# A hybrid retention, latent-attention and expert layer: the order of steps, heads, router, branch and last pair is changed, and the last norm is shared out differently

## The chip, the core and the metric

The kernel runs on one core of a Trainium2 chip. Its engines are TensorE (PE in the profile; its weight loads are PEld), VectorE (DVE), ScalarE (ACT), GpSimd (POOL) and SyncE (SP, which issues nearly all loads). The metric is the device time of one execution in microseconds; lower is better.

## The reference

One layer for 256 latent tokens of width 2048 and 256 context tokens, in fp32. Cut to what matters here:

```python
mod_x = split(silu(c) @ w_ada + b_ada, 6)          # modulations 0 to 5; mod_c for the context
proj = modulate(x, mod_x[0], mod_x[1]) @ w_in      # q, k, v, g, latents; for the context too
ret = retention_output(bidirectional_retention(rope(q), rope(k), v), g)   # 8 heads
att = block_attention(latent queries, latent keys and values)              # 8 heads
mix = concat([ret, att]) @ w_o
h = layer_norm(ALPHA * x + mod_x[2] * mix)
y = hier_moe(modulate(h, mod_x[3], mod_x[4]))      # 4 groups x 8 experts, each token in 2
out = layer_norm(ALPHA * h + mod_x[5] * y)
```

`hier_moe` picks one group and two experts of it for each token. The 32 experts' weights are 403 MB of fp32.

## The kernel before

The program is written as one stream of operations; a planner (priority by place in the program, with modelled durations) sets the order in which each engine issues them, except where an order is pinned. No order is pinned in the kernel before.

**Input projection (L567 to L636).** The rows of the weight are taken in six stages of 1, 1, 2, 4, 4 and 4 blocks of 128 (`STAGES`). Within a stage the ten column blocks of 512 (`NB_TO`) come as chunks of about 1 MB, in the order that `win_chunks` gives (L47); blocks 2, 3, 4, 5 and 9 are computed for latent and context tokens (four row tiles), the others for the latent ones (two). A chunk is split into a rounded high and a low part (`split_w`: ScalarE copies, VectorE subtracts, L273 and L274, two buffers), and each product is three TensorE products (L594 to L596). Chunks stream through four buffers (`st`). Between chunks run *pieces* of the product that gives modulations 0 and 1 for the next stage (`gemv_plan`, L510 to L543): one piece is one modulation's share of a chunk of rows, with its own load in `st`; the even and odd rows of modulation m go to column groups 2m and 2m+1 of one bank. They are spread over the chunks by L604.

**Modulation steps (`ada_step`, L243).** Modulations 2 to 5 are summed by VectorE: 64 steps, each a 1 MB load (`sa`, two buffers) and two operations on 128x1024 (L250). `ada_v` holds 48 of them (modulations 3, 4, 2) and `ada_g` 16 (modulation 5). `ADA_V` places them behind chunks, `ADA_V_MLA` in the attention, `ADA_G_WO` in the output projection. `ada_finish` (L210) sums modulations 3 and 4 over partitions with 16 one-column products each.

**Retention.** In the last stage k is rotated on GpSimd behind chunk 3, q on VectorE behind chunk 5, and there also all eight heads are written (`ret_tables`, `ret_head`, L347 to L408). `mla_latents` follows at chunk 8, then the norm and output of retention, then the attention.

**Output projection and router (L842 to L912).** Four blocks of 512 columns, 16 chunks. The products of the router with the not yet normalised rows are accumulated on the way (`router_part`); `router_consts` makes on GpSimd four weighted copies of the router's weights and sums them on VectorE (L810). After the last block come mean and variance, the router's logits, the choice of group and experts (L942 to L954), the places of tokens (L956 to L970), and `norms` (L925), which makes the normalised rows in high and low parts for the gather.

**Experts (L1190 to L1241).** 16 pairs. Expert weights are loaded 2 MB at a time into six buffers, five ahead (`expert_chunk`). For each expert the tokens' rows are gathered by products with 0/1 matrices (`gather_two`, L1049), multiplied by gate and up (L1071) and down (L1116), scaled by their gates in a high and a low part (`down`, L1122 and L1123), and scattered back by two products (`scatter`, L1130), multiplied by modulation 5 (L1131) and added to h (L1132). Behind the sixth pair (`pr == 5`) a branch handles experts that got more tokens than their 64 places (`overflow`, L1134); it is not taken in the profiled execution.

**Last norm (L1243 to L1254).** Statistics, then eight pieces: VectorE takes six of them in two operations each (L181, L182), ScalarE and GpSimd the two others (L184 to L186); each piece is stored when ready.

## Time and profile before

| | |
|---|---|
| time, median of 3 runs | 1685.78 us (1684.48 to 1687.98) |
| profiled execution, time | 1686.18 us |
| profiled execution, span | 1684.4 us |
| mean granted TensorE clock | 0.972 of full |
| TensorE busy (with pipelined ends) | 1521.6 us, 90% |
| VectorE busy | 919.9 us, 55% |
| ScalarE busy | 484.2 us, 29% |
| GpSimd busy | 105.9 us, 6% |
| HBM read and written | 575.8 and 2.1 MB, 343 GB/s over the span |

The span runs from the first to the last instruction of one execution. Engine shares over the whole span mix stages with different limits, so they are read by stage. A matmul's recorded duration contains its pipeline's end; the step from one start to the next is its price in a row of them.

### The profile page before, as it was taken

Reading aid. Unit: us, or ns where it says so; the run is one execution under the profiler, and the core shown is the slowest. Engines: PE = TensorE matmul, PEld = TensorE weight load, DVE = VectorE, ACT = ScalarE, POOL = GpSimd, SP = SyncE. Lnnn points to the kernel's source line nnn. Section 1 sums busy time; section 2 is a strip of 40 time slices with the busy share of each in tenths; the row PEclk is TensorE's granted clock in tenths of the full one; section 3 lists DMA queues with packets and bytes.
Section 4 is the critical chain, followed back from the end, with each engine's and each line's share of the span. In section 5 each row is a group of like instructions: output and inputs, shape, how many; then the busy total and the mean of one; then the engine's idle time right before and its main releaser. Section 6 shows DMA issues by size and latency. Waiting matters only on the chain. (4 is left out here: it accounts for less than half of the span.)

```text
span 1684.4 us, 20454 instructions
## 1 busy us (share of the span) xinstructions
PE 1521.6 (90%) x8316; PEld 919.2 (55%) x8316; DVE 919.9 (55%) x1553; ACT 484.2 (29%) x913; POOL 105.9 (6%) x91
## 2 busy tenths in 40 slices
PE   5999999988889999699999988799989989899994
PEld 4667686877768767444543543444445345336432
DVE  6877584899698768824423532432342343234238
ACT  3323232324675534431320211121122013103112
POOL 1000000053513010000000000000000000000001
PEclk8999999998999999899999999999999999999997
DMA  8787777766554579579999999999999999999993
GB/s 326 272 326 283 294 309 286 276 245 225 184 192 153 199 270 360 225 301 426 426 427 427 426 427 425 370 428 427 427 427 427 427 426 427 426 426 427 421 425 136
DMA packets 54226, 579.28 MB, mean 344 GB/s; under 512 B 6320, under 2 KB 6768, under 8 KB 8816
## 3 DMA queue, kind: packets, MB, share of 16 engines
q1 hardware_dynamic: 54000, 577.90, 84.2%
q8 instruction: 67, 1.10, 0.3%
q14 instruction: 31, 0.25, 0.0%
q0 software_dynamic: 128, 0.03, 0.0%
HBM read 575.81 MB, written 2.10 MB: 343 GB/s over the span
## 5 line engine op out<-in xcount | busy, mean ns | idle before, releaser
L1071 PE MATMUL pA<-we,xg 128*64 128x512 f32 x2048 | 468.0, 602 | 12.8 <-DMA we<-in_wexp_dram 12.8
L1071 PEld LDWEIGHTS pA<-we,xg 128*64 128x64 f32 x2048 | 140.8, 138 | 281.2 <-issue 247.6
L1116 PE MATMUL pA<-we,hT 128*64 128x256 f32 x2048 | 232.7, 382 | 17.4 <-DMA we<-in_wexp_dram 16.1
L1123 DVE SCALAR_TENSOR_TENSOR D<-pA,gcol,D 64x256 fp32r<-64x256 f32 x256 | 123.5, 482 | 176.0 <-ACT D L1122 175.3
L273 ACT CAST whi<-st 128x1024 fp32r<-128x1024 f32 (+3 forms) x130 | 125.1, 965 | 282.5 <-PE pA L596 172.5
L1116 PEld LDWEIGHTS pA<-we,hT 128*64 128x64 f32 x2048 | 147.4, 137 | 92.2 <-ACT D L1122 8.7
L595 PE MATMUL pA<-wlo,xhi 128*128 128x512 f32 (+1 forms) x480 | 188.2, 392 | 10.5 <-DVE wlo L274 10.5
L594 PE MATMUL pA<-whi,xhi 128*128 128x512 f32 (+1 forms) x480 | 185.5, 394 | 3.3 <-ACT whi L273 3.1
L596 PE MATMUL pA<-whi,xlo 128*128 128x512 f32 (+1 forms) x480 | 185.8, 387 | 0.0
L250 DVE SCALAR_TENSOR_TENSOR ada_acc<-st,c,ada_acc 128x1024 f32<-128x1024 f32 x128 | 177.5, 1406 | 8.3 <-DMA st<-in_ada_dram 8.2
L274 DVE TENSOR_TENSOR wlo<-st,whi 128x1024 fp32r<-128x1024 f32 (+2 forms) x122 | 134.6, 1112 | 57.6 <-ACT whi L273 57.1
L1122 ACT ACTIVATE D<-pA,gcol 64x256 fp32r<-64x256 f32 x256 | 120.0, 469 | 156.7 <-PE pA L1116 87.5
L1074 ACT ACTIVATE hid<-pA 128x256 f32<-128x256 f32 x32 | 12.3, 383 | 493.5 <-PE pA L1071 493.5
L1075 DVE TENSOR_TENSOR hid<-pA,hid 128x256 f32<-128x256 f32 x32 | 13.5, 423 | 219.7 <-ACT hid L1074 219.7
L594 PEld LDWEIGHTS pA<-whi,xhi 128*128 128x128 f32 x480 | 90.5, 191 | 37.5 <-ACT whi L273 17.7
L595 PEld LDWEIGHTS pA<-wlo,xhi 128*128 128x128 f32 x480 | 91.9, 191 | 31.9 <-DVE wlo L274 14.5
L1058 DVE TENSOR_SCALAR xg<-pT,modt 128x256 f32<-128x256 f32 x64 | 34.8, 544 | 131.2 <-PE pA L1071 93.7
L1131 DVE TENSOR_TENSOR pA<-pA,ada_acc 128x512 f32<-128x512 f32 x128 | 83.5, 693 | 36.8 <-PE pA L1130 36.6
L596 PEld LDWEIGHTS pA<-whi,xlo 128*128 128x128 f32 x480 | 92.0, 192 | 16.3
L1049 PE MATMUL pT<-oh,nn 128*128 128x256 f32 x512 | 80.5, 303 | 9.1 <-DVEq L1136 5.8
L1049 PEld LDWEIGHTS pT<-oh,nn 128*128 128x128 f32 x512 | 68.3, 199 | 31.7 <-issue 20.5
L1132 DVE TENSOR_TENSOR h<-pA,h 128x512 f32<-128x512 f32 x128 | 82.6, 683 | 0.8
(353 smaller groups left out, 1578.6 us busy)
## 6 DMA issues: line engine op xcount, KB each, us to landing
we<-in_wexp_dram SPq DMA_DIRECT2D x190, 2048.0 KB, 21.8
st<-in_ada_dram SPq DMA_DIRECT2D x96, 1024.0 KB, 6.7
st<-in_win_dram SPq DMA_DIRECT2D x35, 1024.0 KB, 6.7
st<-in_wo_dram SPq DMA_DIRECT2D x16, 1024.0 KB, 4.9
we<-in_wexp_dram SPq DMA_DIRECT2D x4, 1024.0 KB, 17.4
st<-in_wuq_dram SPq DMA_DIRECT2D x3, 1024.0 KB, 4.8
xn<-in_x_dram SPq DMA_DIRECT2D x2, 1024.0 KB, 6.4
xn<-in_ctx_dram SPq DMA_DIRECT2D x2, 1024.0 KB, 17.0
```

The costliest lines, as they stand in the source:

```text
L250: V.scalar_tensor_tensor(accs[m][:, sl], w[:, sl], c2[:, k, 0:1], accs[m][:, sl], op0=OP.mult, op1=OP.add)
L273: A.copy(hi, src)
L274: (eng or V).tensor_tensor(lo, src, hi, op=OP.subtract)
L594: T.matmul(banks[t][:, :wd], xh[:, sl], hi[:, kk, :wd], start=fst, stop=False)
L595: T.matmul(banks[t][:, :wd], xh[:, sl], lo[:, kk, :wd], start=False, stop=False)
L596: T.matmul(banks[t][:, :wd], xl[:, sl], hi[:, kk, :wd], start=False, stop=lst)
L1049: T.matmul(p[:, 256 * j:256 * j + width], nnh[i % 2][:, i // 2, ks], oh[:, i // 2, :width], start=(i == 0), stop=(i == 3))
L1071: T.matmul(pg[64 * cg:64 * cg + 64], xg[:, k, c0:c0 + 64], c[:, kk, 512 * cg:512 * cg + 512], start=(k == 0), stop=(k == KB - 1))
L1116: T.matmul(pd[64 * cg:64 * cg + 64, :256], hT[:, f % 2, 64 * (f // 2):64 * (f // 2) + 64], c[:, f, 256 * cg:256 * cg + 256], start=(f == 0 ...
L1122: A.activation(hl[0][rows, sl], p, AF.Copy, scale=g)
L1123: V.scalar_tensor_tensor(hl[1][rows, sl], p, g, hl[0][rows, sl], op0=OP.mult, op1=OP.subtract)
L1131: V.tensor_tensor(p, p, mod5[:, sl], op=OP.mult)
```

## The change

- Pieces of modulations 0 and 1 come as pairs: one piece loads both modulations' chunks and alternates their products. In the long stages the pieces stand behind chunks 1, 3, 4, 5 and 6. The first stage's pieces keep their written order on TensorE.
- Between the first and last stage the column blocks alternate between those without and with context.
- `ada_finish` for modulations 3 and 4 uses four 512-wide products and transposes.
- The step lists are 50 and 14 long; `ADA_V` places 23 before the last stage and 10 in it.
- k is rotated on VectorE. Tables for two heads come behind chunk 5; behind chunks 6 to 9 come two heads each, with the tables for the next two.
- The router's four sums stand behind four different chunks. From the last projection block to the last normalised part VectorE, ScalarE and TensorE issue in written order; the transposes come first, the two square roots are split from their reciprocals, the two halves of the tokens alternate in the choice, and the norm of the last three quarters comes behind the places.
- The router's weights are queued behind the last normalised part on ScalarE.
- The branch stands ahead of the sixth pair's down products; that pair's scatter and next gather follow as in every other pair.
- In the last pair `down` multiplies by gate and modulation 5 in one operation into one fp32 tile, and `scatter` is one fp32 product.
- The last norm: for columns 0 to 1023 VectorE does the first operation, TensorE multiplies by the inverse deviation (a diagonal) and adds the shift, ScalarE copies out; for the others VectorE does both. GpSimd has no part.

```diff
-ADA_V = [[0] * 10, [0] * 10, [0] * 5, [1] * 10, [1] * 10, [2] * 4 + [1] * 6]
+ADA_V = [[0] * 3, [1, 0, 0], [1, 1, 1, 0, 1], [1] * 7 + [0, 1, 1], [1] * 7 + [0, 1, 1], [1] * 10]
+GEMV_AT = (1, 3, 4, 5, 6)
...
+    elif si:
+        order = [0, 2, 1, 3, 6, 4, 7, 8, 5, 9]
...
-    ada_v = [(m, k) for m in (3, 4, 2) for k in range(KB)]
-    ada_g = [(5, k) for k in range(KB)]
+    ada_g = [(m, k) for m in (3, 4, 2, 5) for k in range(KB)]
+    ada_v = [ada_g.pop(0) for _ in range(50)]
...
-            for k in range(KB):
-                T.matmul(p[:, k:k + 1], acc[:, 128 * k:128 * k + 128], ones[:, 0:1], start=True, stop=True)
...
+            for g in range(4):
+                T.matmul(p[32 * g:32 * g + 32], ones[:, 0:32], acc[:, 512 * g:512 * g + 512], start=True, stop=True)
+            row = sa.tile([128, 2048], F32, name="st", tag="st")[:, :512]
+            A.copy(row, p)
+            p = bankT()
+            for j in range(4):
+                transpose(p[:, 128 * j:128 * j + 128], row[:, 128 * j:128 * j + 128])
...
-                c = stream(dram2(a["ada01"], base + (m * nch + j) * 128 * per * w, 128, per * w), per * w)
+                c = [stream(dram2(a["ada01"], base + (m * nch + j) * 128 * per * w, 128, per * w), per * w)
+                     for m in range(2)]
                 for kk in range(per):
                     k = j * per + kk
-                    g = 2 * m + (k % 2)
-                    T.matmul(p[32 * g:32 * g + 32, :w], csil[:, k], c[:, kk * w:kk * w + w],
-                             start=(k < 2), stop=(k >= KB - 2))
+                    for m in range(2):
+                        g = 2 * m + (k % 2)
+                        T.matmul(p[32 * g:32 * g + 32, :w], csil[:, k], c[m][:, kk * w:kk * w + w],
+                                 start=(k < 2), stop=(k >= KB - 2))
...
+            if nchunk == 10:
+                n = GEMV_AT.count(ci)
...
-                            rope(pl["k"][:, t, 512 * j:512 * j + 512], t, "ck", "sk", 4, 64, R["rt"], G)
+                            rope(pl["k"][:, t, 512 * j:512 * j + 512], t, "ck", "sk", 4, 64, R["rt"])
...
-                    for h in range(H):
+                    for h in range(2):
                         ret_tables(h)
+                if ci > 5:
+                    for h in range(2 * ci - 12, 2 * ci - 10):
                         ret_head(h)
+                        if h < H - 2:
+                            ret_tables(h + 2)
...
+                if 1 <= 4 * n + k4 <= 4:
+                    router_const(4 * n + k4 - 1, rparts[4 * n + k4 - 1])
...
+        pinned = tc.manual_schedule(engines={V.engine, A.engine, T.engine})
+        pinned.__enter__()
+        flipped = [router_flip(3, half) for half in range(2)]
         for half in range(2):
-            router_part(3, half)
+            router_rest(3, half, flipped[half])
...
+        norm_a(0, 0)
+        norm_a(1, 0)
+        V.reciprocal(hs[:, :, 1:2], hs[:, :, 1:2])
+        norm_b(0, 0)
+        norm_b(1, 0)
...
+    norm_a(1, 1)
     for t in range(2):
+        V.scalar_tensor_tensor(rk[:, t], p[:, 32 * t:32 * t + 32], 1.0, sel[:, t], op0=OP.add, op1=OP.mult)
+        normed_lo(t, 0, fs[t])
...
     oh = new_places(0)
-    norms()
+    for c in range(1, 4):
+        for t in range(2):
+            if c > 1:
+                norm_a(t, c)
+            norm_b(t, c)
+            done, f = normed(t, c)
+            normed_lo(t, c, f)
...
+            if len(hl) == 1:
+                V.scalar_tensor_tensor(hl[0][rows, sl], p, g, mod5[rows, 512 * n + 256 * cg:512 * n + 256 * cg + 256],
+                                       op0=OP.mult, op1=OP.mult)
...
+            if len(hl) == 1:
+                T.matmul(p, sT[:K, t, :].bitcast(F32), hl[0][:K], start=True, stop=True)
...
         if pr == 0:
-            router_weights()
+            with tc.issue_after(done.ins):
+                router_weights()
...
-        hl = new_D()
-        gather = pq and not final and pr != 5
+        if pr == 5:
+            overflow()
+        hl = new_D_whole() if final else new_D()
+        gather = pq and not final
...
-        if pr == 5:
-            for n in range(4):
-                scatter(hl[n], sT, 128, n)
-            hl = None
-            overflow()
...
+    for t in range(2):
+        for n in range(2):
+            p = shifted[t, n] = bankA()
+            T.matmul(p, ones[0:1], lnb[0:1, 512 * n:512 * n + 512], start=True, stop=False)
...
+    for n in range(4):
+        sl = slice(512 * n, 512 * n + 512)
+        for t in range(2):
+            hp = h[:, t, sl]
+            if n < 2:
+                T.matmul(shifted[t, n], diag[:, t], hp, start=False, stop=True)
+                A.copy(hp, shifted[t, n])
+            else:
+                affine(V, hp, mv2[:, t, 0:1], mv2[:, t, 2:3], lnw[:, sl], lnb[:, sl], None)
+            SP.dma_start(out[128 * t:128 * t + 128, sl], hp)
```

## Rows read from the trace of the kernel before

**Rows 1.** Windows: us; PE, PEld, DVE, ACT, POOL busy; clock, DMA share, GB/s.

```profile
126.00:337.00 211.00, 211.00 (x1009) 156.82 (x1008) 148.56 (x179) 61.27 (x87) 2.30 (x2) 1.00 0.75 290
337.00:404.00 67.00, 61.17 (x256) 49.12 (x255) 63.24 (x91) 20.78 (x33) 30.34 (x28) 0.95 0.68 246
404.00:490.00 86.00, 71.93 (x406) 61.45 (x405) 71.10 (x150) 59.01 (x142) 38.06 (x32) 0.92 0.55 197
490.00:600.00 110.00, 100.28 (x542) 81.76 (x540) 89.48 (x147) 58.82 (x112) 23.71 (x15) 0.98 0.49 185
...
741.00:1653.00 912.00, 838.22 (x4913) 407.40 (x4910) 329.28 (x626) 177.35 (x379) 0.00 (x0) 0.99 1.00 422
1653.00:1684.40 31.40, 7.12 (x44) 3.85 (x42) 27.45 (x44) 6.39 (x12) 5.95 (x4) 0.66 0.19 67
```

**Rows 2.** Waits of the load queue (SP): total us, times, longest.

```profile
SPq L1030 <- PE pA L1071: 554.1, 124, 31.9
...
SPq L142 <- PE pG L526: 150.6, 26, 10.9
...
SPq L1136 <- SPq L1136: 24.4, 6, 4.9
```

**Rows 3.** Timeline of TensorE, one piece and two together: start, us.

```profile
192.89 0.39 PE L595 MATMUL pA<-wlo,xhi 128*128 128x512 f32 x1
193.12 0.39 PE L596 MATMUL pA<-whi,xlo 128*128 128x512 f32 x1
193.44 1.91 PE L526 MATMUL pG<-st,csil 128*32 128x512 f32 x8
...
245.15 1.94 PE L526 MATMUL pG<-st,csil 128*32 128x512 f32 x16
```

**Rows 4.** Windows of line 526 alone, pieces of three stages, summed.

```profile
sum 159.00, PE 38.85 PEld 8.01; mean PE 12.95 PEld 2.67
```

**Rows 5.** Groups by line and shape, 0 to 600 us: busy us, mean ns.

```profile
L215 PE MATMUL pT<-ones,ada_acc 128*128 128x1 f32 x64 | 8.0, 258 | 1.0 <-ACT qk L388 1.0
...
L661 PE MATMUL pA<-st,cqall 128*128 128x512 f32 x16 | 7.2, 593 | 0.0
```

**Rows 6.** Instructions of two tiles (k, then q): ns min/median/max.

```profile
L317 POOL TENSOR_TENSOR lk<-lk,rp1p x4: 726/1222/1717, 352.2 to 377.1; 128x256 f32<-128x256 f32 x4
...
L317 DVE TENSOR_TENSOR lq<-lq,rp x4: 417/418/419, 401.4 to 409.3; 128x256 f32<-128x256 f32 x4
```

**Rows 7.** Timeline of TensorE: the heads' first wait, their last product.

```profile
408.13 0.47 PE L169 MATMUL pT<-ct,lq 128*128 128x128 f32 x1 [3.79 <-DVE lq L317]
...
458.06 0.61 PE L404 MATMUL pA<-Ssb,xq 128*128 128x128 f32 x4
```

**Rows 8.** Windows of line 250 (modulation steps) alone.

```profile
400.00:490.00 90.00, 36.52 (x25) 0.92 0.56 199
```

**Rows 9.** Timeline of TensorE, start of the output projection.

```profile
601.66 0.80 PE L853 MATMUL pA<-wlo,mix 128*128 128x512 f32 x1 [4.13 <-DVE wlo L274]
```

**Rows 10.** Timeline of VectorE, then TensorE, from projection to gather.

```profile
689.74 0.70 DVE L871 TENSOR_TENSOR pA<-pA,ada_acc 128x512 f32<-128x512 f32 x1 [1.77 <-PE pA L854]
...
700.07 0.75 DVE L182 SCALAR_TENSOR_TENSOR h<-h,hs,D 128x512 f32<-128x512 f32 x1
...
712.78 0.24 DVE L954 SCALAR_TENSOR_TENSOR sel<-ct,ef,o 128x32 f32<-128x32 f32 x1
...
713.53 4.09 PE L1049 MATMUL pT<-oh,nn 128*128 128x256 f32 x16
```

**Rows 11.** Windows: the worst 5 us of the stream, at the branch.

```profile
1070.00:1075.00 5.00, 2.98 (x14) 3.01 (x15) 2.09 (x4) 0.26 (x1) 0.00 (x0) 0.50 0.69 213
```

**Rows 12.** Groups by line on VectorE from 1640 us on.

```profile
L182 DVE SCALAR_TENSOR_TENSOR h<-h,mv,lnwb 128x512 f32<-128x512 f32 (+1 forms) x6 | 6.1, 1058 | 0.0
L1131 DVE TENSOR_TENSOR pA<-pA,ada_acc 128x512 f32<-128x512 f32 x8 | 5.6, 694 | 0.1
```

**Rows 13.** Page, load issues: KB each, median us to landing.

```profile
st<-in_wuq_dram SPq DMA_DIRECT2D x3, 1024.0 KB, 4.8
```

More of the change, by code (lines that the diff above doesn't have):

```diff
@@ L515, in gemv_plan, with piece @@
         base = sum(2 * D * n * 128 for _, n in STAGES[:si])
-        def piece(j, m):
+        def piece(j):
             def go():
@@ L540, in gemv_plan @@
         for j in range(nch):
-            pieces.append(piece(j, 0))
-            pieces.append(piece(j, 1))
+            pieces.append(piece(j))
         return pieces + [last]
@@ L558, in xhat @@
         V.tensor_tensor(lo[:, sl], full, hi[:, sl], op=OP.subtract)
-    for f in gemv_plan(0):
-        f()
-    for k in range(STAGES[0][1]):
-        xhat(k, 0)
+    with tc.manual_schedule(engines={T.engine}):
+        for f in gemv_plan(0):
+            f()
+        for k in range(STAGES[0][1]):
+            xhat(k, 0)
     SP.dma_start(rot["t"], a["consts"][:, CW:CR])
@@ L956, in tile_kernel @@
-    p = bankA()
-    T.matmul(p[:, 0:32], C("ut"), sel[:, 0], start=True, stop=True)
-    V.scalar_tensor_tensor(rk[:, 0], p[:, 0:32], 1.0, sel[:, 0], op0=OP.add, op1=OP.mult)
-    p = bankA()
-    T.matmul(p[:, 0:32], ones, sel[:, 0], start=True, stop=False)
-    T.matmul(p[:, 0:32], C("ut"), sel[:, 1], start=False, stop=True)
-    V.scalar_tensor_tensor(rk[:, 1], p[:, 0:32], 1.0, sel[:, 1], op0=OP.add, op1=OP.mult)
+    Le = [L[:, t, 8:40] for t in range(2)]
+    fs = [normed(t, 0)[1] for t in range(2)]
@@ L979, in tile_kernel @@
     oh = new_places(0)
-    norms()
+    for c in range(1, 4):
+        for t in range(2):
+            if c > 1:
[3 more added lines that the diff above has]
+            normed_lo(t, c, f)
     nnfs.close()
@@ L983, in tile_kernel @@
         f()
+    pinned.__exit__(None, None, None)
     def router_weights():
@@ L1108, in new_D, with new_D_whole @@
         return [[D2[j][:, n] for j in range(2)] for n in range(4)]
+    def new_D_whole():
+        D1 = dp.tile([128, 4, 512], F32, name="D0")
+        return [[D1[:, n]] for n in range(4)]
     def down(hT, src, hl, gcol, half, n):
```

127 lines of the change are left out of this document (73 added, 54 removed).

## The prediction

> **What bounds the kernel now.** I read the busy times by stage first [rows 1], then for each stage what the engine with the least slack waits for. From 741 to 1653 us the kernel streams expert weights: the DMA share is 1.00 at 422 GB/s, while TensorE is 838 of 912 us busy [rows 1]. Nothing in the change lessens those bytes. So this stage can only start earlier; and it starts when TensorE has worked through the first expert's gate and up product, because its reads free the ring buffers: the load queue waits longest for them [rows 2]. What is saved before 741 moves the whole stream, one for one, and so does what is saved after 1653.
>
> From 126 to 337 us TensorE is busy all 211 us at full clock while VectorE has 30% to spare and the DMA 25% [rows 1]: TensorE sets that stretch. From 337 to 600 no engine is full: TensorE 233 of 263 us, VectorE 224. There chains between engines decide, and the granted clock falls to 0.92 in the heads (404 to 490). From 600 to 691 the output projection runs, on TensorE again; from 691 to 741 first a chain of small VectorE work, then TensorE. After 1653 VectorE works 27.5 of 31.4 us.
>
> The sum is made against the profiled execution: span 1684.4 us, time 1686.2 us, which is 0.4 us above the median of the runs. It carries over as it is.
>
> **The modulation pieces.** A piece today is one modulation's share: in the last stages 8 recorded products, 1.91 us. Where the planner happened to set two pieces side by side, 16 products took 1.94 us [rows 3], since the two modulations write different column groups of one bank. The change makes every piece such a pair. The three stages with 512-wide pieces spend 38.85 us on 192 products [rows 4]; 12 pairs of 1.94 us are 23.3 us, which saves 15.6 us of TensorE. Two of the three windows lie where TensorE has no other slack; I take **-12**, bounds -16 and 0. What hides it if wrong: nothing, it is on the path; what can eat it is loading (rival 2), as a pair holds two of the four stream buffers and the queue already waits 150.6 us in sum for pieces to free one [rows 2].
>
> **Modulation 3 and 4 finish.** 64 products of one column, 8.0 us in both finishes [rows 5], become 16 recorded 512-wide fp32 products over four column groups and 8 transposes. The nearest price is 7.2 us for 16 full-width fp32 products [rows 5]; side by side as in a pair of pieces a quarter, 1.8 us. With about 1 us of transposes that is 2.8 to 8.2 us against 8.0. I lean to the overlapped end because the pieces show it: **-3**, bounds -5 and +0.5. A copy on ScalarE and a borrowed step buffer come on top, off the path.
>
> **Rotation of k from GpSimd to VectorE.** On GpSimd the 24 operations take 0.73 to 1.7 us each; on VectorE the same form takes 0.418 us [rows 6], so 24 add 10 us to an engine that has 4 us free from 337 to 404 [rows 1]. GpSimd's last of them starts at about 377; k is wanted by the heads only after 404. Operations of VectorE beside GpSimd are stretched (1.06 for 0.75 us in the tail, below), so part of the 10 comes back. I take **0**, bounds -5 and +5.
>
> **Heads.** Today all eight heads run ahead of the last four weight chunks: from 404 to 490 TensorE is busy 71.9 us of 86 [rows 1], and it begins with 3.79 us behind the rotation of q [rows 7]; the last head ends at 458.7. The change sets two heads behind each of the last four chunks, so a chunk's products can fill the heads' waits. TensorE's own floor is 71.9 us at clock 0.92, some 66 us at full clock: at best -20. ScalarE has 59 us of work there, so it does not forbid that. VectorE does in part: 71 us, of which 36.5 us are modulation steps [rows 8]. The new plan puts 10 steps into this whole last stage, 23 before it and 17 behind it; the old plan 14 here. So VectorE gets lighter here and heavier in the attention that follows (89.5 of 110 us). If the last two heads end up alone behind the last chunk, a chain of about 6 us (50 us for eight heads) is bare. I take **-8**, bounds -20 and +4, and for the moved steps 0, bounds -3 and +5.
>
> **Start of the output projection.** TensorE waits 4.13 us [rows 9], because VectorE's four sums for the router stand, in order, before a weight split and themselves wait for GpSimd. One sum per chunk instead lets the splits pass: **-3**, bounds -4 and 0.
>
> **Router.** Between the last projection's product and the first gather VectorE is never idle: 689.74 to 713.0 [rows 10]. The short chain (scale, variance, logits, maxima) is threaded with norm operations of 0.7 us that the first gather does not need (rows 10 show one of four between the logits and the second square root, at 700.07; five more of them and three low parts stand before the last choice at 712.78). The pinned order moves most of them behind. Walking it with today's durations: the two mean-and-scale products and the transposes end at 692.9, statistics at 695.2, the first norm quarter at 698.5, logits and variance at 701, gate inputs at 702.6, the ten choice operations for both halves in turn (about 2.6 us) at 705.2, ranks and two low parts at 707.6, places at 708.3. Today's gather starts at 713.53 [rows 10], so -5.2. Behind it six norm pieces follow, each with VectorE waiting some 1.4 us for ScalarE. TensorE needs 24 us for this expert anyway, so they just keep ahead of it. I take **-5**, bounds -8 and +2.
> The Trainium skill (TensorE: Matmul & The Clock Gate, on engine queue depths) says ScalarE and VectorE are strict FIFO, so everything behind a waiting low part waits too. By that rule alone the six waits, 8 us, would turn this term to +3 and the time to 1657; the rows show VectorE waiting in order but not what the planner threads into the gaps.
>
> **Branch.** The overflow test moves ahead of the sixth pair's down products. Today the queue waits 24.4 us in all there for loads to land, and the stream falls to 213 GB/s in the worst 5 us [rows 2, 11]; the drain belongs to the branch and stays. Scatter and gather get back beside other work, which the DMA hides: **-0.5**, bounds -5 (no drain) and +3.
>
> **Tail.** In the last pair the eight multiplications by modulation 5 (5.6 us) leave VectorE [rows 12]; the down products' second operation takes it in. A scatter is one fp32 product (two records of 0.45 us [rows 5]) for two of 0.23, the step of that shape [rows 3]: +0.9 us per block on TensorE, four blocks, the first three mostly behind VectorE. The norm's 12 operations run at 1.06 us beside GpSimd against 0.75 us alone [rows 10, 12]; again there are 12, without GpSimd: some 3.5 us less. Half of the second steps go to TensorE, at half clock there (granted 0.66 over the tail), four fp32 products of up to 1.8 us, and ScalarE copies. VectorE saves 9 us, TensorE's scatters and the ScalarE end give 3 back: **-6**, bounds -9 and -2.
>
> **Start.** The pinned order interleaves two loads, the second of which lands later: 0, bounds -1 and +2.5.
>
> Sum: -12 -3 -8 -3 -5 -0.5 -6 = **-37.5 us, 1649 us**.
>
> **Rivals.**
> 1. *VectorE takes over.* It is 85% busy from 337 to 600, with 10 us added; if its order becomes the bound, heads and finishes gain nothing and three quarters of the pieces' gain is given back as waits for weight splits: -37.5 + 8 + 3 + 9 = -17.5, **1669 us**. For it: 3.8 free of 67 us from 337 to 404. Against: 30% free before 337, fewer steps in the heads.
> 2. *The stream buffers starve* (slower). A pair and the next chunk are 3 MB, 7.4 us at the 422 GB/s of rows 1; a narrow chunk is 24 products of 0.23 us (the step in rows 3), 5.4 us. If the load can only start as the pair ends, with 2.3 us of latency (a lone 1 MB load lands after 4.8 us [rows 13], 2.5 of them transfer) TensorE waits some 4.3 us per pair: 12 x 4.3 = 52, with the gain of 12 lost: -37.5 + 12 + 52 = +26.5, **1713 us**. It makes the kernel slower from 2.1 us of wait per pair on. Against: the narrow and wide chunks now alternate, and the DMA has 25% free.
> 3. *The order does not take* (heads stay in a block, the norm's waits stall the gather): terms of heads and router 0, **1662 us**.
>
> **Chances.** Forecast 0.66; rival 1 0.14; rival 3 0.12; rival 2 0.06; clearly below 1632, 0.02. The terms' half-widths, taken as independent, add up to some 12 to 13 us (the heads' 12 leads): the forecast alone is 1636 to 1661. The range takes in rivals 1 and 3: 1632 to 1675. About 0.2% (3.4 us) is what a measurement here can tell from no change; faster 0.92, same 0.02, slower 0.06.
>
> **What would show it.** Pieces: 16 products together 12 times, about 23 us, and a shorter stretch to the end of the fifth stage by 8 to 14 us. Heads: weight products between head products, the stretch 404 to 490 in under 80 us. Output projection: no 4 us wait at its start. Router: last projection product to first gather in 17 us, not 22. Branch: still a dip of the stream. Tail: last landing to the end in 25 us, not 31. I am wrong if TensorE shows waits for loads or splits from 126 to 337, or if the attention grows by what the heads gave.

## The result and the profile after

The changed kernel takes **1663.78 us** (median of four runs, 1663.34 to 1665.07) against 1685.64: a ratio of **0.987, 95% interval 0.9853 to 0.9887**. The forecast was 1649, with a range of 1632 to 1675. So the direction was right and the time lies in the range, but 15 us of the gain of 37 did not come, and the time lies above the 1636 to 1661 that the prediction gave the forecast alone. The profiled execution took 1665.07 us with a span of 1663.3; the comparison below is of spans, 1684.4 to 1663.3, that is -21.1.

The windows of the profile after, cut where a stage ends (end of the third, fourth and fifth stage of the weight projection; first head product; start of the latent attention; its last product; last output projection product; first gather; last load landed). Columns as in [rows 1].

```profile
87.89:146.14 58.25, 54.15 (x263) 37.98 (x263) 40.60 (x57) 16.74 (x27) 0.00 (x0) 0.94 0.79 306
146.14:238.98 92.84, 92.82 (x450) 69.45 (x449) 65.86 (x77) 27.11 (x37) 0.00 (x0) 1.00 0.74 283
238.98:331.77 92.79, 91.92 (x462) 69.95 (x461) 63.14 (x77) 27.54 (x38) 2.29 (x2) 1.00 0.74 291
331.77:391.93 60.16, 59.04 (x268) 48.75 (x268) 57.66 (x115) 20.38 (x30) 6.09 (x4) 1.00 0.66 248
391.93:463.37 71.44, 61.10 (x359) 51.30 (x358) 60.84 (x128) 55.90 (x134) 38.84 (x32) 0.98 0.48 177
463.37:567.21 103.84, 91.01 (x485) 74.50 (x484) 90.84 (x154) 57.33 (x114) 16.70 (x6) 0.92 0.55 203
567.21:675.98 108.77, 103.56 (x464) 77.67 (x463) 82.60 (x83) 38.30 (x43) 7.08 (x8) 1.00 0.80 308
675.98:693.23 17.25, 9.04 (x44) 4.47 (x43) 15.77 (x70) 6.84 (x12) 0.00 (x0) 0.96 0.78 334
693.23:1636.46 943.23, 872.75 (x5050) 425.95 (x5051) 347.66 (x665) 195.30 (x402) 0.00 (x0) 0.98 0.98 414
1636.46:1663.30 26.84, 18.56 (x60) 7.54 (x58) 18.73 (x35) 2.82 (x6) 0.00 (x0) 0.83 0.24 78
```

The same marks in the trace of before give these lengths (us), with the forecast's terms set beside them:

| stretch | before | after | difference | forecast |
|---|---|---|---|---|
| start to end of second stage | 90.11 | 87.89 | -2.2 | pieces, start |
| third stage | 53.09 | 58.25 | **+5.2** | pieces |
| fourth and fifth stage | 195.37 | 185.63 | -9.7 | pieces, one finish |
| *sum to here* | 338.57 | 331.77 | **-6.8** | -13.5 |
| to the start of the latent attention | 149.29 | 131.60 | **-17.7** | -9.5 |
| latent attention | 94.71 | 103.84 | **+9.1** | 0 |
| output projection | 108.51 | 108.77 | +0.3 | -3 |
| to the first gather | 22.45 | 17.25 | -5.2 | -5 |
| first gather to last load | 940.07 | 943.23 | **+3.2** | -0.5 |
| last load to the end | 30.80 | 26.84 | -4.0 | -6 |

Four places carry most of the miss of 16.4 us: the third stage, the attention (which took back half of what the heads gave), the output projection's start and the first expert; 2 us more are the tail's. The experiments go through them in order.

### The profile page after: what moved, and what is told of

It reads as the page before. It is cut to its first block, busy times and chain, and to the rows that moved or that the text cites. A ratio compares the mean times of both kernels' runs of the same rounds, so it can differ in the third digit from the quotient of the medians.

```text
span 1663.3 us, 20393 instructions
## 1 busy us (share of the span) xinstructions
PE 1521.9 (92%) x8292; PEld 912.9 (55%) x8292; DVE 911.5 (55%) x1569; ACT 479.8 (29%) x903; POOL 76.6 (5%) x63
## 5 line engine op out<-in xcount | busy, mean ns | idle before, releaser
L1130 PE MATMUL pA<-we,xg 128*64 128x512 f32 x2048 | 469.8, 606 | 12.5 <-DMA we<-in_wexp_dram 11.3
L1191 DVE SCALAR_TENSOR_TENSOR D<-pA,gcol,D 64x256 fp32r<-64x256 f32 x240 | 115.8, 483 | 175.3 <-ACT D L1190 174.7
L604 PE MATMUL pA<-wlo,xhi 128*128 128x512 f32 (+1 forms) x480 | 186.8, 389 | 3.5 <-DVE wlo L281 3.5
L603 PE MATMUL pA<-whi,xhi 128*128 128x512 f32 (+1 forms) x480 | 183.3, 396 | 4.5 <-ACT whi L280 4.4
L257 DVE SCALAR_TENSOR_TENSOR ada_acc<-st,c,ada_acc 128x1024 f32<-128x1024 f32 x128 | 172.5, 1364 | 7.7 <-DMA st<-in_ada_dram 7.7
L1190 ACT ACTIVATE D<-pA,gcol 64x256 fp32r<-64x256 f32 x240 | 112.5, 469 | 147.6 <-PE pA L1180 85.9
L1134 DVE TENSOR_TENSOR hid<-pA,hid 128x256 f32<-128x256 f32 x32 | 13.5, 422 | 221.6 <-ACT hid L1133 221.6
L603 PEld LDWEIGHTS pA<-whi,xhi 128*128 128x128 f32 x480 | 90.1, 192 | 35.7 <-ACT whi L280 15.2
L604 PEld LDWEIGHTS pA<-wlo,xhi 128*128 128x128 f32 x480 | 91.9, 192 | 25.6 <-DVE wlo L281 6.4
L1203 DVE TENSOR_TENSOR pA<-pA,ada_acc 128x512 f32<-128x512 f32 x120 | 77.9, 693 | 40.4 <-PE pA L1201 40.4
L1108 PEld LDWEIGHTS pT<-oh,nn 128*128 128x128 f32 x512 | 68.4, 198 | 34.0 <-issue 17.7
```

The costliest lines, as they stand in the source:

```text
L257: V.scalar_tensor_tensor(accs[m][:, sl], w[:, sl], c2[:, k, 0:1], accs[m][:, sl], op0=OP.mult, op1=OP.add)
L603: T.matmul(banks[t][:, :wd], xh[:, sl], hi[:, kk, :wd], start=fst, stop=False)
L604: T.matmul(banks[t][:, :wd], xh[:, sl], lo[:, kk, :wd], start=False, stop=False)
L1108: T.matmul(p[:, 256 * j:256 * j + width], nnh[i % 2][:, i // 2, ks], oh[:, i // 2, :width], start=(i == 0), stop=(i == 3))
L1130: T.matmul(pg[64 * cg:64 * cg + 64], xg[:, k, c0:c0 + 64], c[:, kk, 512 * cg:512 * cg + 512], start=(k == 0), stop=(k == KB - 1))
L1190: A.activation(hl[0][rows, sl], p, AF.Copy, scale=g)
```

## Experiments

All are the changed kernel with the difference shown (`...` marks lines left out); a window's sum line covers all of its stretches, and a line number is that of the run's own kernel. Times are medians; the ratio is to the kernel before on the same chip, and the changed kernel's is 0.987. Single runs lie up to 4.7 us from their median (e7), so where a few us matter the length of the stretch in the trace decides. By itself such a length varies too. In the traces whose code is the same there, the third stage takes 57.2 to 58.4 us, the way from the end of the fifth stage to the end of the attention 234.3 to 235.7 (e4: 240.5), the output projection 108.7 to 111.1, first gather to last load 942.0 to 943.2, and the tail 26.6 to 28.1.

**The third stage.** Here TensorE waits 4.1 us, before 1.1. Its timeline in the changed kernel, and that of the load queue (start, duration); L535 are the pieces, L544 their finish, L173 transposes, L603 and L604 weight products:

```profile
109.69 4.38 PE L535 MATMUL pG<-st,csil 128*32 128x512 f32 x32
114.79 1.05 PE L544 MATMUL pG<-ct,row 128*128 128x4 f32 x8 [0.72 <-ACT row L541]
116.71 0.89 PE L173 MATMUL pT<-ct,xn 128*128 128x128 f32 x4 [0.87 <-ACT xf L564]
118.58 1.15 PE L173 MATMUL pT<-ct,xn 128*128 128x128 f32 x4 [0.97 <-ACT xf L564]
120.57 2.17 PE L603 MATMUL pA<-whi,xhi 128*128 128x512 f32 x4 [0.85 <-ACT whi L280]
122.54 0.63 PE L604 MATMUL pA<-wlo,xhi 128*128 128x512 f32 x1
...
93.10 11.19 SPq L146 DMA_DIRECT2D st<-in_ada_dram  x5
111.66 11.61 SPq L146 DMA_DIRECT2D st<-in_win_dram  x5
```

Two pairs (32 products) stand together; five pieces and steps in a row were loaded ahead of the next weight chunk, which was issued only at 111.66, when a pair gave its buffers back. That chunk landed at 118.55. Behind the wait a product takes 0.63 us instead of 0.39 (granted clock 0.50 from 120 to 125 us, the level of 1.2 GHz).

```diff
             if nchunk == 10:
                 n = GEMV_AT.count(ci)
+            if nchunk == 5:
+                n = (2, 1, 1, 1, 0)[ci]
```

> The changed kernel with one difference: in the third stage (five chunks) the four paired pieces and the finish stand 2, 1, 1, 1 behind the chunks instead of 2, 2, 1. Theory A (stream buffers): in the changed kernel two pairs held all four stream buffers from 101.3 to 114.1 us, the next weight chunk was issued at 111.7 and landed at 118.6, and TensorE waited, at half clock until 125. With a chunk's load between the pairs the third stage ends at 141 us or before instead of 146.1, the end of the fifth stage comes 4 to 6 us earlier, and the whole run takes 1658 to 1660 us instead of 1663.8. Theory B (the finish chain, that is the copy of the sums, the transposes and the scaled input, is what TensorE waits for, whatever is loaded): the same 3.4 us of waits stand later in the stage, and the run stays at 1662 to 1665.

Measured: 1661.48 us, ratio 0.9852 (0.9831 to 0.9874), 1.5 us above A's range. The third stage takes 54.12 us, and in the profile the fifth ends 5.3 us earlier, 1.1 of it gained ahead of the third stage, where nothing differs; 3.5 reach the end of the expert stream (the output projection varies by 2 us). Its pairs now stand singly, and of the waits the two behind ScalarE's scaled input are gone:

```profile
98.27 1.92 PE L535 MATMUL pG<-st,csil 128*32 128x512 f32 x16
108.57 1.92 PE L535 MATMUL pG<-st,csil 128*32 128x512 f32 x16
118.85 1.92 PE L535 MATMUL pG<-st,csil 128*32 128x512 f32 x16
121.50 1.05 PE L544 MATMUL pG<-ct,row 128*128 128x4 f32 x8 [0.73 <-ACT row L541]
```

Theory A holds for the stretch. The finish chain is the same, so B falls.

**What a pair is worth.** First each piece by itself, one modulation's load and products and then the other's, but in the same places:

```diff
-                for kk in range(per):
-                    k = j * per + kk
-                    for m in range(2):
+                for m in range(2):
+                    c = stream(dram2(a["ada01"], base + (m * nch + j) * 128 * per * w, 128, per * w), per * w)
+                    for kk in range(per):
+                        k = j * per + kk
                         g = 2 * m + (k % 2)
```

> The changed kernel with each modulation piece worked off by itself again, in the same places and the same order of loads. Theory A (the pair is worth its TensorE time): each pair of 1.92 us becomes two pieces of 1.91, so the fourth and fifth stage take 4 us longer each, the third about as much, and the run 1672 to 1676. Theory B (the pairs lose in loads what they save in products, as the third stage seemed to show): the run stays within 3 us of 1663.8.

Measured: 1673.97, ratio 0.9933 (0.9914 to 0.9952). But the fourth and fifth stage take 92.71 and 92.54 us, as in the changed kernel, and the trace says why: two pieces that stand next to each other overlap without being threaded.

```profile
193.37 1.94 PE L534 MATMUL pG<-st,csil 128*32 128x512 f32 x16
```

So the theories were not told apart, and that the time lies in A's range is chance. The profiled execution lost 8.7 us elsewhere: 2.6 in the first three stages and 5.0 from the fifth stage to the attention's end (240.5 us instead of 235.4). There the same program came out in another order, with the first head product 65.5 us behind the fifth stage instead of 60.2; why is not shown. The second run sets the pieces one behind each chunk:

```diff
-        def piece(j):
+        def piece(j, m):
...
-            pieces.append(piece(j))
+            pieces.append(piece(j, 0))
+            pieces.append(piece(j, 1))
...
-            if nchunk == 10:
-                n = GEMV_AT.count(ci)
```

> The changed kernel with the pieces single and one behind each chunk, as in the kernel before (the run in which they were single but stood side by side took 1.94 us for 16 products all the same, so it undid nothing of the overlap). Theory A (adjacency is what makes a pair cheap): the fourth and fifth stage take some 96 us each instead of 92.8, the third stage, whose loads are then mixed again, 53 to 55 instead of 58.3, and the run 1665 to 1668. Theory B (the pieces hide under loads or VectorE anyway): the fourth and fifth stage stay at 93 us and the run is under 1663.

Measured: 1675.06, ratio 0.9938 (0.9922 to 0.9955), 7 us above A's range; the profiled run 1672.65. Line of the pieces alone, windows by stage (us; PE, PEld; clock, DMA share, GB/s):

```profile
147.80:244.40 96.60, 14.44 (x64) 2.85 (x64) 1.00 0.74 290
244.40:341.00 96.60, 13.40 (x64) 2.72 (x64) 1.00 0.72 280
```

and in the changed kernel, with its third stage first:

```profile
86.00:115.00 29.00, 9.48 (x64) 2.00 (x64) 1.00 0.83 320
146.10:239.00 92.90, 10.81 (x64) 2.04 (x64) 1.00 0.74 283
239.00:331.80 92.80, 8.74 (x64) 1.79 (x64) 1.00 0.74 291
```

Theory A for these two stages: 3.6 and 4.7 us less on TensorE are 3.7 and 3.8 us less in the stages. Up to the end of the second stage the pairs gain 3.4 us (91.30 to 87.89). In the third stage the single pieces are faster by 1.7 us (56.55 to 58.25), but not in the 53 to 55 that A gave them. The fourth stage's pieces gain less on TensorE than the fifth's because not every pair stayed whole; one pair of the changed kernel:

```profile
190.84 1.05 PE L535 MATMUL pG<-st,csil 128*32 128x512 f32 x2
192.40 1.92 PE L535 MATMUL pG<-st,csil 128*32 128x512 f32 x14
```

In five of the twelve pairs (one in the third stage, three in the fourth, one in the fifth) the first two recorded products stand apart like this, and the pair costs 3 us instead of 1.92.

**Heads, rotation, steps.** From the end of the fifth stage to the end of the attention the changed kernel takes 235.4 us, before 244.0. Four runs change one thing each there.

```diff
-                    for h in range(2):
+                    for h in range(H):
                         ret_tables(h)
-                if ci > 5:
-                    for h in range(2 * ci - 12, 2 * ci - 10):
                         ret_head(h)
```

> The changed kernel with the eight retention heads back in one block behind the sixth chunk. Theory A (the interleaving is what shortened this stretch): from the first head product to the start of the attention it takes some 84 us instead of 71.5, and the run 1674 to 1677. Theory B (VectorE's lighter load there, 29 step records from 337 us on instead of 42, shortened it): the stretch grows by less than 4 us and the run stays under 1668.

Measured: 1678.19, ratio 0.9957 (0.9942 to 0.9971). Both theories fall in their letter: up to the start of the attention it takes 130.2 us, 1.4 less than interleaved, but the attention then takes 111.4 and the output projection 116.7 instead of 108.8. The cost of a block of heads comes out behind it, in steps that were put off: 32 step records in the attention instead of 29 and 25 in the projection instead of 22.

```diff
-    rope(pl["k"][:, t, 512 * j:512 * j + 512], t, "ck", "sk", 4, 64, R["rt"])
+    rope(pl["k"][:, t, 512 * j:512 * j + 512], t, "ck", "sk", 4, 64, R["rt"], G)
```

> The changed kernel with the rotation of k back on GpSimd. Theory A (VectorE bounds the stretch from the end of the fifth stage to the end of the attention, 209 of 235 us busy): VectorE has 24 operations of 0.42 us less, though its others run slower beside GpSimd; the stretch takes 228 to 234 us and the run 1656 to 1662. Theory B (the operations that GpSimd slows cost more than the move saves): it takes 236 to 241 us and the run 1664 to 1669.

Measured: 1670.58, ratio 0.9907 (0.9891 to 0.9924). The stretch takes 241.93 us: theory B. Modulation steps alone, in the parts of the stretch (us; VectorE busy and count), first the part ahead of the heads with the rotation on GpSimd and one step out of it, then the three parts in the changed kernel:

```profile
331.43:399.22 67.79, 23.32 (x16) 0.95 0.59 220
...
359.83 1.83 DVE L257 SCALAR_TENSOR_TENSOR ada_acc<-st,c,ada_acc 128x1024 f32<-128x1024 f32 x1
```

```profile
331.77:391.93 60.16, 16.35 (x13) 1.00 0.66 248
391.93:463.37 71.44, 23.82 (x16) 0.98 0.48 177
463.37:567.21 103.84, 44.18 (x29) 0.92 0.55 203
```

Beside GpSimd's rotation a step record takes 23.32/16 = 1.46 us on average, without it 1.26. Record by record it is plainer: of these 16 the seven that overlap GpSimd's work by more than a sliver take 1.38 to 1.83 us, the others 1.27 to 1.29. In the heads and in the attention GpSimd has other work in both kernels, and there the changed kernel's records average 1.49 and 1.52 too.

```diff
-ADA_V = [[0] * 3, [1, 0, 0], [1, 1, 1, 0, 1], [1] * 7 + [0, 1, 1], [1] * 7 + [0, 1, 1], [1] * 10]
+ADA_V = [[0] * 10, [0] * 10, [0] * 5, [1] * 10, [1] * 10, [2] * 4 + [1] * 6]
-    ada_v = [ada_g.pop(0) for _ in range(50)]
+    ada_v = [ada_g.pop(0) for _ in range(48)]
```

> The changed kernel with the table of modulation steps of the kernel before (ten in each of the fourth and fifth stage, fourteen in the sixth, none in front). Theory A (the new table pushed steps out of the heads and into the attention, 29 records there instead of 18, which is what the attention's 9 us more are): the attention is back at 84 to 88 us from its first latent product on, the stretch from the end of the fifth stage to the end of the attention takes 229 to 232 us instead of 235.4, and the run 1658 to 1661. Theory B (the place of a step does not matter, VectorE has the same sum from the fifth stage on): the stretch stays within 2 us and so does the run. Theory C (the new table is a gain: steps in front are hidden, the old one has more of them behind): the stretch takes 238 us or more and the run over 1666.

Measured: 1671.0, ratio 0.9904 (0.9877 to 0.9931). Counted from its first latent product, the attention is back at 84.9 us (changed kernel 89.9, before 84.75), as A said, but the stretch takes 241.64: theory C. The part ahead of the heads grew by 9.8 us.

```diff
-ADA_V = [[0] * 3, [1, 0, 0], [1, 1, 1, 0, 1], [1] * 7 + [0, 1, 1], [1] * 7 + [0, 1, 1], [1] * 10]
+ADA_V = [[0] * 3, [1, 0, 0], [1, 1, 1, 0, 1], [2] * 3 + [1] * 7, [2] * 3 + [1] * 7, [1] * 10]
-ADA_V_MLA = 2
+ADA_V_MLA = 1
```

> The changed kernel with seven modulation steps moved from the attention (one step a head instead of two) into the fourth and fifth stage (13 each instead of 9). Theory A (VectorE's order bounds the attention): the attention took 94 us before with 18 step records and 103.4 us after with 29; with some 14 fewer it takes 93 to 96 us, the two stages in front, where VectorE has a quarter of its time free, stay within 2 us, and the run takes 1655 to 1659. Theory B (the longer attention is its granted clock, 0.92 after and 0.98 before, or the bare end of the heads): the attention stays over 100 us and the run at 1662 to 1666. Theory C (the loads of the moved steps starve the paired pieces): the fourth and fifth stage take 5 us or more longer and the run 1664 or more.

Measured: 1664.72, ratio 0.9881 (0.9863 to 0.99). The stretch falls by 5.6 us, to 229.80; the fifth stage grows by 5.9 us, to 98.69, with one wait of TensorE for a late weight chunk:

```profile
289.10 1.22 PE L603 MATMUL pA<-whi,xhi 128*128 128x512 f32 x2 [3.52 <-ACT whi L280]
```

So A holds for the stretch, though not for the attention alone (101.7 us, where the chain ahead of its first latent product grew to 17.4 us, from 14.0), C holds for the fifth stage, and they cancel. The sums of the windows over the stretch, in the order kernel before, heads in a block, steps of before, steps early (the changed kernel's rows stand above: 209.3 of 235.4 us on VectorE; with the rotation on GpSimd it is 213.2 of 241.9):

```profile
sum 244.00, PE 216.85 PEld 179.16 DVE 211.60 ACT 131.65 POOL 85.03; mean PE 72.28 PEld 59.72 DVE 70.53 ACT 43.88 POOL 28.34
```

```profile
sum 241.57, PE 215.51 PEld 176.16 DVE 205.10 ACT 131.65 POOL 55.76; mean PE 107.76 PEld 88.08 DVE 102.55 ACT 65.83 POOL 27.88
```

```profile
sum 241.64, PE 210.91 PEld 172.97 DVE 215.44 ACT 132.76 POOL 58.38; mean PE 70.30 PEld 57.66 DVE 71.81 ACT 44.25 POOL 19.46
```

```profile
sum 229.80, PE 207.46 PEld 171.56 DVE 202.62 ACT 133.22 POOL 64.00; mean PE 103.73 PEld 85.78 DVE 101.31 ACT 66.61 POOL 32.00
```

VectorE's idle time is what one looks at here: 26.1 us in the changed kernel, 28.7 with the rotation on GpSimd, 26.2 and 27.2 with the other tables of steps; but 36.5 with the heads in a block and 32.4 before. With the heads interleaved the stretch is VectorE's work plus some 27 us, whatever stands where; over all twelve traces with interleaved heads it is VectorE's work plus 24.4 to 28.7. TensorE's busy time does not follow the length: it stays at 207 to 212 us in these traces, while the length goes from 229.8 to 241.9. That VectorE sets this stretch is a reading of these sums. The steps moved early (e2) come nearest to changing VectorE's work alone: 6.7 us less of it, and a stretch 5.6 us shorter.

**Start of the output projection.** TensorE's waits there, and what VectorE does:

```profile
584.28 0.50 PE L876 MATMUL pA<-wlo,mix 128*128 128x512 f32 x1 [3.15 <-DVE wlo L281]
587.94 0.50 PE L876 MATMUL pA<-wlo,mix 128*128 128x512 f32 x1 [0.63 <-DVE wlo L281]
...
577.98 1.42 DVE L827 TENSOR_REDUCE rc<-st 128x40 f32<-128x640 f32 x1
581.18 1.40 DVE L827 TENSOR_REDUCE rc<-st 128x40 f32<-128x640 f32 x1 [1.78 <-POOL st L821]
582.50 1.73 DVE L281 TENSOR_TENSOR wlo<-st,whi 128x1024 fp32r<-128x1024 f32 x1
```

Two sums still stand ahead of the split, one waiting for GpSimd: 3.78 us in all, before 4.13 [rows 9].

```diff
-                if 1 <= 4 * n + k4 <= 4:
-                    router_const(4 * n + k4 - 1, rparts[4 * n + k4 - 1])
-                if n == 1 and k4 == 2:
+                if 4 <= 4 * n + k4 <= 7:
+                    router_const(4 * n + k4 - 4, rparts[4 * n + k4 - 4])
+                if n == 2 and k4 == 0:
```

> The changed kernel with the router's four sums three chunks of the output projection later. Theory A (a sum still stands in front of a weight split and waits 1.78 us for GpSimd's product, so the first wait of the projection only shrank from 4.13 to 3.15 and 0.63 us): with the products long done the waits go, the projection takes 105 to 106 us instead of 108.8, and the run 1660 to 1662. Theory B (the split waits for ScalarE's copy or for the modulation steps, whatever the sums do): the projection stays over 108.

Measured: 1667.77, ratio 0.9896 (0.9879 to 0.9912), the projection 109.53 us. The planner put the sums where they were:

```profile
578.90 1.40 DVE L827 TENSOR_REDUCE rc<-st 128x40 f32<-128x640 f32 x1 [1.77 <-POOL st L821]
```

TensorE's wait is there as before (3.14 us), so this run did not test the theories. Its median is 4.0 us above the changed kernel's all the same, while its profiled run is the lowest of the four (1663.12, the others 1667.7 to 1668.9); what the others lost is not shown. The next one holds each sum behind VectorE's latest weight split:

```diff
+            lastv["ins"] = done.ins
...
+                if 4 <= 4 * n + k4 <= 7:
+                    with tc.issue_after(lastv["ins"]):
+                        router_const(4 * n + k4 - 4, rparts[4 * n + k4 - 4])
...
```

> The changed kernel with the router's four sums held, on VectorE's own queue, behind the weight splits of the fifth to eighth chunk of the output projection (moving them in the program alone had left them at the same place, 2 to 3 us behind GpSimd's products). Theory A (the sum's wait for GpSimd in front of a split is what TensorE waits for): the waits of 3.15 and 0.63 us go, the projection takes 105 to 106.5 us instead of 108.8, and the run 1660 to 1662. Theory B (the split is late for another reason): the projection stays over 108.

Measured: 1664.74, ratio 0.9868 (0.9841 to 0.9895). The waits at the start are gone (the 25th recorded product of each chunk's third kind, line 877 in the changed kernel, starts 18.0 us behind the first, not 20.8), but the projection takes 109.74 us:

```profile
618.98 0.30 PE L173 MATMUL pT<-ct,h 128*128 128x128 f32 x1 [1.84 <-DVE h L902]
621.81 0.80 PE L880 MATMUL pA<-wlo,mix 128*128 128x512 f32 x1 [1.77 <-DVE wlo L283]
```

The sums now stand between splits and norm work, the last at 613 us, and TensorE waits some 35 us later than before; that the sums cause this wait is read from the order and not tested. Over the whole projection it waits 4.8 us, in the changed kernel 5.2. A holds for the first wait and fails for the time.

**First expert.** The gather starts 17.25 us behind the last product instead of 22.45 [rows 10]. Then VectorE stands behind ScalarE in five of the norm pieces, and gathers stand behind these; behind its first gather TensorE waits 1.8 us in this expert, in the kernel before 0.03:

```profile
693.23 3.75 PE L1108 MATMUL pT<-oh,nn 128*128 128x256 f32 x16 [2.01 <-DVE oh L1020]
715.89 0.50 PE L1108 MATMUL pT<-oh,nn 128*128 128x256 f32 x2 [0.71 <-ACT nn L978]
...
700.35 0.69 DVE L982 TENSOR_TENSOR nn<-nnf,nn 128x512 fp32r<-128x512 f32 x1 [1.53 <-ACT nn L978]
```

```diff
+    late_lo = []
...
             done, f = normed(t, c)
-            normed_lo(t, c, f)
+            if late_lo:
+                normed_lo(*late_lo.pop())
+            late_lo.append((t, c, f))
+    normed_lo(*late_lo.pop())
```

> The changed kernel with one difference behind the first gather: each low part of a norm piece is taken one piece later, so that VectorE multiplies the next piece while ScalarE makes this one's high part. Theory A (VectorE standing in order behind ScalarE, 1.53 us a piece, holds the first expert's gathers): the last gate product of the first expert comes 24 us or less after the first gather instead of 28.8, the expert stream and its end follow by 1.5 to 3 us, and the run takes 1661 to 1662. Theory B (TensorE's half clock at its start, or the loads, set that stretch): it stays within 1 us.

Measured: 1660.6, ratio 0.9849 (0.9833 to 0.9866). VectorE's waits of 1.53 us are gone (one of 0.93 is left), the 64th gate product ends 27.1 us behind the first gather (28.8), and to the last load it takes 940.52 us instead of 943.23. That is theory A in direction and size, with 2.7 us against the changed kernel's trace and 1.5 against the shortest of the other traces (942.03); A's 24 us to the last gate product did not come.

**Tail.** The last load lands at 1636.46; TensorE's last scatters, VectorE's last statistic and ScalarE's last copy:

```profile
1641.30 3.70 PE L1198 MATMUL pA<-D,sT 128*128 128x512 f32 x8
1646.18 1.27 DVE L1253 BATCH_NORM_STATS2 st<-h 128x6 f32<-128x512 f32 x2
1656.29 0.58 ACT L1333 COPY h<-pA 128x512 f32<-128x512 f32 x1 [0.27 <-PE pA L1332]
```

```diff
-            SP.dma_start(out[128 * t:128 * t + 128, sl], hp)
+            (A if n < 2 else SP).dma_start(out[128 * t:128 * t + 128, sl], hp)
```

> The changed kernel with the four outputs that ScalarE copies issued from ScalarE's queue instead of SyncE's. Theory A (the last norm ends 24.6 us earlier than before and the last output lands only 21.1 earlier, since eight issues of 0.4 to 0.9 us stand in line on one queue): the last output is issued at 1656.5 instead of 1658.3, lands 1.5 to 2 us earlier against the last load, and the run takes 1661.5 to 1663. Theory B (2 MB in 9 us are the writes' own rate): the landing moves by less than 0.5 us.

Measured: 1664.16, ratio 0.9856 (0.9831 to 0.9881). From the last load to the end it takes 26.27 us, only 0.6 less than the changed kernel; by its letter A is not met, nor is B. But the last copy itself comes later in this trace, and the last output lands sooner behind it:

```profile
1658.63 0.58 ACT L1333 COPY h<-pA 128x512 f32<-128x512 f32 x1 [0.57 <-PE pA L1332]
...
1659.24 0.34 ACTq L1336 DMA_DIRECT2D out_dram<-h  x1
```

The last output is issued 0.03 us behind the end of that copy and lands 3.6 us behind it; in the changed kernel it is issued 1.5 us and lands 5.4 us behind the copy, and in all twelve other traces with one queue it lands 5.2 to 5.4 behind. The copy is late because TensorE's products ahead of it run longer at the lower clock (granted 0.51, about the level of 1.2 GHz, in the 6.4 us from 14 us behind the last load on, in the changed kernel 0.69). In e1, e4 and e9 the clock does the same, the last copy comes at the same 21.6 us behind the last load, and the tail takes 27.95 to 27.98. Against these, two queues save 1.7 us, which is A's size: the line of issues did hold the end. It is one trace, and the median does not show it.

**Both mends together.**

> The changed kernel with two differences at once: the paired pieces of the third stage spread over its chunks, and the low parts of the norm pieces taken one piece later. Theory A (two separate waits, one at 110 us and one behind 693 us, so they add): in the profiled execution the third stage ends 4 us or more earlier and the stretch from the first gather to the last load lands at 940.5 us instead of 943.2; with 2.3 and 3.2 us by the medians of the single runs the run takes 1657 to 1659.5 us. Theory B (what the front gains is given back to VectorE before the stream, as the weight projection gave back the wait that the pinned sums saved): the run takes 1660 to 1662, no better than the second difference alone.

Measured: **1658.26 us** (1656.71 to 1659.6), ratio **0.9834 (0.9812 to 0.9857)**; every run lies below every run of the changed kernel. Windows of the third stage, and from the first gather to the last load:

```profile
86.79:141.01 54.22, 52.61 (x264) 36.82 (x263) 38.58 (x55) 16.63 (x27) 0.00 (x0) 0.97 0.82 311
688.11:1628.21 940.10, 868.24 (x5050) 420.38 (x5051) 347.27 (x665) 195.83 (x402) 0.00 (x0) 0.99 0.99 416
```

Theory A: 5.1 us up to the first gather, 3.1 from there to the last load.

## Why the prediction was right in direction and too large

The range held because it took in the rivals: 1663.78 lies between rival 3 (1662) and rival 1 (1669), outside the 1636 to 1661 of the forecast alone. That inner range was added up wrongly. The half-widths as given, taken as independent, make 17.8 us and not 12 to 13, so it should have read 1631 to 1667. Both of my signs of being wrong came in part: TensorE waited 0.85 us for a split in the fifth stage, and the attention grew by half of what the heads gave.

**Pieces (-12, bounds -16 and 0).** A whole pair costs what I forecast, 1.92 us, but five of the twelve were not whole. The 192 wide products of the three stages fell from 39.3 us of TensorE (the windows of [rows 4] miss 0.5 of it) to 29.0, -10.3 where 15.6 were worked out. The narrower pieces of the start gave 6.2 more (19.76 to 13.57 up to 86 us), which the sum did not have; that the two make 16.5 together is chance. Taking all pairs apart costs 7.6 us in the profiled runs and 11.3 by the medians. The failed sentence is "the narrow and wide chunks now alternate": that is so in the stages of ten chunks, and the third has five. There rival 2 came true, in one place: two pairs held the four buffers, and 4.1 us went (58.25 to 54.12 in e1). I had priced it per pair for all twelve and given it 0.06 as a whole, instead of asking in which stage it could happen. Even with single pieces the third stage takes 56.55 us (e8), before 53.09. The column order and four modulation steps behind its chunks are new there, and no run separates them.

**Finish (-3).** The fifth stage, where the first lies, gained 6.03 us, 3.81 of it the pairs': 2.2 are left for one finish, though that stage's steps changed too. TensorE's own rows fit: eight recorded products of 1.04 us and transposes of 0.60, where 30 of the 32 old products took 3.49. The second lies among the heads and was not measured apart.

**Rotation (0, bounds -5 and +5).** On GpSimd it costs 6.5 us of the stretch: outside my bounds. I had counted 10 us of VectorE against a stretching that I saw only in the tail. The row of the steps [rows 8] shows such a stretching too, beside GpSimd's other work there: 36.52 us for 25 records is 1.46 each, where a whole one takes 1.27 alone. The Trainium skill (SBUF — State Buffer, Who interferes with whom) says that a VectorE instruction with two SBUF inputs contends with a GpSimd instruction that reads SBUF; the trace agrees, 1.46 to 1.26 in e5 and the changed kernel.

**Heads (-8) and moved steps (0, bounds -3 and +5).** Up to the attention -17.7 instead of -9.5, in the attention +9.1, outside the bounds; together -8.56, near the sum of the forecast by cancelling, which is luck. (Where the border lies is partly chance too: in the other traces that keep this stretch at 234 to 236 us, the attention takes 100.7 to 103.2, with more time ahead of it.) What failed is the frame: I priced heads, rotation and steps as terms that add. Undone one at a time they cost 6.1, 6.5 and 6.2 us of this stretch, 18.8 in sum, where all together, with the second finish, brought 8.56; besides, a single edit makes the planner put off other steps. One sum for the stretch fits every run with interleaved heads: VectorE's busy time plus 24 to 29 us. By that sum rival 1 (VectorE takes over) was right about the bound and wrong that the gain is then lost: interleaving took 6 to 10 us out of VectorE's idle time, and that is most of the gain. One reading was loose: the output projection of the kernel before starts at 582 us, not 600, so the "89.5 of 110 us" of the attention holds 18 us of it.

**Output projection (-3).** It gave +0.3, and TensorE's waits in it add up to 5.2 us, before 4.8. "One sum per chunk instead lets the splits pass" failed: the planner decides where a sum stands, and its place in the program did not move it (e7). Rival 3, the order does not take, was true here. Held back (e10), the wait came up again 35 us later.

**Router (-5).** The walk gave a gather at 708.3 against 713.53; it came 5.2 us earlier relative to the last product. But "they just keep ahead of it" failed: VectorE waited 6.0 us for ScalarE in five pieces, and 1.5 to 2.7 us of it reached the stream (e6), so the term is some -3. The strict order that the Trainium skill states (TensorE: Matmul & The Clock Gate, engine queue depths) is what the rows show here; of the 8 us that I had worked out from it, these 1.5 to 2.7 reached the time.

**Branch (-0.5).** It holds as far as the stream shows it. The stream still falls, at the load queue's branch, and now in two slices:

```profile
1020.00:1025.00 5.00, 3.08 (x17) 1.16 (x13) 0.42 (x1) 0.38 (x1) 0.00 (x0) 1.00 0.24 95
1025.00:1030.00 5.00, 2.55 (x9) 1.83 (x11) 0.54 (x1) 0.94 (x2) 0.00 (x0) 0.64 0.93 324
```

Against 422 GB/s that is 5 x (327 + 98)/422 = 5.0 us of stream; before, with 292, 213 [rows 11] and 295, 5.5.

**Tail (-6, bounds -9 and -2).** -4.0. The last statistic ends 11.0 us behind the last load, before 15.1, and the last copy another 9.4, before 12.1 to VectorE's last operation: -6.8. The norm's operations take 0.74 us, as said, where [rows 12] have 1.06. But the last output lands 5.4 us behind the last copy (1662.29 to 1656.87), before 2.6. I had left out the writes: eight outputs, 2.1 MB, go out within 8.8 us, before within 11.7, and the last one's issue now stands 1.5 us in line behind the others. With a second queue 1.8 of the 2.8 us went (e11).

**Start (0).** It gave -2.2. With single pieces the changed kernel takes 91.3 us there (e8), before 90.1: so the pairs brought 3.4, and what took back 1.2 is not shown.

## What to carry to other kernels

Where two engines trade work in one stretch, do not add up edits: sum the busy time of the fullest engine over the whole stretch, see how much it idles and why, and price an edit by what it does to these two. A group of loads that belongs together needs a look at every stage's own order: how many buffers it holds while the next weight chunk waits to be issued. Before a chain is shortened by moving it in the program, see who sets the order there: the planner put one back (e7), and held in place it gained nothing (e10). And when the last results come closer together, look at the queue that issues their writes: compare from the last result to the last landing, since the clock ahead of it can hide the difference (e11).

## What the runs showed that was not expected

GpSimd's rotation of k slows VectorE by more than it relieves it: with 24 operations less, VectorE was busy 64.7 us ahead of the heads instead of 57.7 (three step records more are 3.8 of it, three operations of q's rotation 1.3). And two groups of products for separate columns overlap when they merely follow each other, 1.94 us for 16 (e4, and [rows 3] already), as when they are threaded, 1.92. A pair with weight products in between costs 3 us, as five of the twelve did.
